# The gated mixing of a gMLP layer in float32r halves, its sample rows in one product over 96 rows

## The chip, the cores and the metric

The kernel runs on one core of a Trainium2 chip. The metric is the device time of one execution in microseconds; a smaller time is better. Times before are the median of three runs.

## The reference, cut to what matters

One inference step of a two-layer encoder over 256 prompt frames and 32 sample frames, 2048 wide. Layer 0 mixes tokens by a gated MLP, layer 1 by retention; each is followed by a SwiGLU feed-forward, and each of the four sublayers by a layer norm. The change lies in layer 0's mixer:

```python
z = jax.nn.gelu(x @ w_in, approximate=False)
u, v = jnp.split(z, 2, axis=-1)
v = layer_norm(v, ln_g, ln_b)
w = jnp.where(mask[None], w_s[:, :seg, :seg], 0.0)     # 8 groups, lower triangular
mixed = jnp.einsum('gts,bnsgc->bntgc', w, vg) + bias   # over the frames of one segment
s = u * mixed.reshape(bsz, t, GMLP_HALF)
return s @ w_out, v
```

A segment is 128 frames: the prompt has two, the sample is a short one of 32 frames. So for each of the 16 blocks of 128 channels there are three products: two of 128 by 128 frames and one of 32 by 32.

## The kernel before

All activations are kept transposed, with channels on the partitions and the 288 frames (256 prompt, 32 sample) along the free axis. The kernel works in float32 by halves: a value f is split into hi, its rounding to float32r, and lo = f - hi. `split` (L407) does this with one ScalarE copy (L408) and one VectorE subtraction (L409). Each 128x128 weight block then takes three float32r matmuls of 288 columns in `Core.step`: hi by x's hi (L98), hi by x's lo (L99), lo by x's hi (L100).

The weights come packed in the order in which they are used, in chunks of 8 blocks (512 KB each). `Core.prep` (L62) loads a chunk into `raw` by the SP queue, and splits it into `whi` and `wlo`. It runs three chunks ahead of use; `raw` has three buffers, `whi` and `wlo` four each. One chunk lasts TensorE 24 matmuls. TensorE's order is the program's order; that of ScalarE (ACT), VectorE (DVE), GpSimd (POOL) and the SP queue is set by a scheduler, and each of them works through its own list strictly in order.

A counter of finished column tiles ("ticks") places side work: `core.after(n, f)` runs f after n more tiles. Four PSUM banks hold column tiles in progress (`acc`), four more serve the side work (`aux`).

The gMLP layer, `gmlp` (L422), goes in this order:

- `tables` (L439) after tick 6: loads the mixing weights `ws` (8 groups, transposed), the mask, the biases, and multiplies mask into `ws` (L445).
- The first 16 column tiles of `a_in` give v. The first four are run as a group, so all four end almost together. `v_evac` (L452) applies Gelu (tile `vg`), transposes 32x32 pieces into `tv`, and after each four tiles `to_rows` (L412) moves the quarter through DRAM into rows: frames on the partitions, in `vp` (prompt, two segments) and `vs` (sample).
- `v_rows` takes statistics (L467), and `v_norm` (L482), once for each quarter of 512 channels, two ticks apart, normalises in place (L489 to L491).
- The next 16 column tiles give u (L497). Five ticks after each, `mix` (L500) forms the three products of its channel block in float32 (L505), adds the bias (L507), multiplies by u (L508) and splits the result into `sh` and `sl` (L511), which feed `a_out`.
- `tv` and `sl` share one piece of memory, `sl` being allocated in `mix(0)`.

`y` holds the input x at the start (it is split into `xh` and `xl`), and from `a_out` on the sums of the residual and layer norm (`PostNorm.part`, L207); in between it is unused.

Of the kernel before, what the change touches and what calls it, by code (L numbers as in the profile page):

```python
# [10 lines left out]
F32 = mybir.dt.float32  # L11
F32R = mybir.dt.float32r
# [7 lines left out]
P = 128  # L20
D = 2048
KT = D // P
NP = 256
NS = 32
NT = NP + NS
NX = NT + 2
NR = 3 * NS
# [132 lines left out]
def rsqrt(nc, out, v, t):  # L160

    nc.vector.tensor_scalar(out.bitcast(I32), v.bitcast(I32), -0.5, float(0x5F3759DF), ALU.mult, ALU.add)
    for _ in range(3):
        newton(nc, out, out, v, t)
# [242 lines left out]
def split(nc, hi, lo, f):  # L407
    nc.scalar.copy(hi, f)  # L408
    nc.vector.tensor_tensor(lo, f, hi.bitcast(F32), ALU.subtract)  # L409


def to_rows(nc, room, src, w, prompt, sample):  # L412


    blocks = room.rearrange("(b s) f -> s b f", s=32)
    for a in range(4):
        nc.gpsimd.dma_start(blocks[:, :, a * w:(a + 1) * w], src[32 * a:32 * a + 32, :, :])
    nc.gpsimd.dma_start(prompt, room[:NP, :].rearrange("(t p) f -> p t f", p=P))
    nc.gpsimd.dma_start(sample, room[NP:, :])


def gmlp(core, cst, x, y, lnp, ins, v_out):  # L422
    tc, nc = core.tc, core.nc
    xh, xl = x
    xs = lambda k: (xh[:, k, :NT], xl[:, k, :NT])
    with ExitStack() as es:
        pool = es.enter_context(tc.tile_pool(name="gm", bufs=1, reuse_waits="tile"))
        sh = pool.tile([P, KT, NT], F32R, name="g_sh")
        tv = pool.tile([P, 4, 9, 4, 32], F32, tag="sl", name="g_tv")
        vp = pool.tile([P, 2, D], F32, name="g_vp")  # L430
        vs = pool.tile([P, D], F32, name="g_vs")
        vt = [vp[:, 0, :], vp[:, 1, :], vs]
        st = pool.tile([P, 3, 4, 6], F32, name="g_st")
        bs = pool.tile([P, 8, NT], F32, name="g_bs")
        ws = pool.tile([P, 8, P], F32, name="g_ws")
        nrm = pool.tile([P, 3, 6], F32, name="g_nrm")
        mask = pool.tile([P, P], F32, name="g_mask")

        def tables():  # L439
            nc.sync.dma_start(ws, ins["wsT"])  # L440
            nc.sync.dma_start(mask, ins["mask"])
            nc.sync.dma_start(bs, ins["a_bs"])
            nc.sync.dma_start(cst["ln"], ins["lnv"])
            for g in range(8):
                nc.vector.tensor_tensor(ws[:, g, :], ws[:, g, :], mask, ALU.mult)  # L445

        core.after(6, tables)
        nc.gpsimd.memset(vs[NS:2 * NS, :], 0.0)
        nc.gpsimd.memset(vs[2 * NS:, :], 0.0)
        rows = [P, P, NS]  # L450

        def v_evac(m, ps):  # L452
            j = m - 16
            vg = pool.tile([P, NT], F32, tag="u", name=f"vg{j}", bufs=8)
            nc.scalar.activation(vg, ps[:, :NT], AF.Gelu)
            q, i = divmod(j, 4)
            nc.vector.transpose(tv[:, q, :, i, :], vg)
            if i == 3:
                t = tv[:, q, :, :, :].rearrange("p b i s -> p b (i s)")
                cs = slice(q * 512, (q + 1) * 512)  # L460
                to_rows(nc, core.room([NT, 512], f"g_room{q}"), t, P, vp[:, :, cs], vs[:NS, cs])
                core.after(2, lambda: v_rows(q))

        def v_rows(q):
            for t in range(3):
                n = rows[t]
                nc.vector.bn_stats(st[:n, t, q, :], vt[t][:n, q * 512:(q + 1) * 512])  # L467
            if q == 3:
                v_stats()

        def v_stats():
            for t in range(3):
                n = rows[t]
                mv = nrm[:n, t, 0:2]
                nc.vector.bn_aggr(mv, st[:n, t, :, :].rearrange("p a b -> p (a b)"))
                nc.vector.tensor_scalar(nrm[:n, t, 2:3], nrm[:n, t, 1:2], LN_EPS, None, ALU.add)
                rsqrt(nc, nrm[:n, t, 3:4], nrm[:n, t, 2:3], nrm[:n, t, 4:5])
                nc.vector.scalar_tensor_tensor(nrm[:n, t, 5:6], nrm[:n, t, 0:1], -1.0, nrm[:n, t, 3:4], ALU.mult, ALU.mult)
            for q in range(4):
                core.after(2 * q, lambda q=q: v_norm(q))  # L480

        def v_norm(q):  # L482
            cs = slice(q * 512, (q + 1) * 512)
            gb = pool.tile([P, 2, 512], F32, tag="gb", name=f"gb{q}", bufs=2)
            nc.sync.dma_start(gb, ins["a_gb"][:, :, cs])
            for t in range(3):
                n = rows[t]
                v = vt[t][:n, cs]
                nc.scalar.activation(v, v, AF.Identity, bias=nrm[:n, t, 5:6], scale=nrm[:n, t, 3:4])  # L489
                nc.vector.tensor_tensor(v, v, gb[:n, 0, :], ALU.mult)  # L490
                nc.vector.tensor_tensor(v, v, gb[:n, 1, :], ALU.add)  # L491
            if q == 3:
                nc.gpsimd.dma_start(v_out, vs[:NS, :])

        def u_evac(m, ps):
            u = pool.tile([P, NT], F32, tag="u", name=f"u{m}", bufs=8)
            nc.scalar.activation(u, ps[:, :NT], AF.Gelu)  # L497
            core.after(5 if m < 14 else 2, lambda: mix(m, u))

        def mix(m, u):  # L500
            g = m // 2
            ps = core.bank(f"mix{m}")
            for t in range(3):
                n = rows[t]
                nc.tensor.matmul(ps[:, t * P:t * P + n], vt[t][:, m * P:(m + 1) * P], ws[:, g, :n], start=True, stop=True)  # L505
            s = pool.tile([P, NT], F32, tag="s", name=f"s{m}", bufs=2)
            nc.vector.tensor_tensor(s, ps[:, :NT], bs[:, g, :], ALU.add)  # L507
            nc.vector.tensor_tensor(s, s, u, ALU.mult)  # L508
            if m == 0:
                late["sl"] = pool.tile([P, KT, NT], F32R, tag="sl", name="g_sl")  # L510
            split(nc, sh[:, m, :], late["sl"][:, m, :], s)  # L511

        late = {}
        core.tiles("a_in", 0, list(range(KT)), list(range(16, 32)), xs, v_evac, lag=0)
        core.tiles("a_in", 0, list(range(KT)), list(range(16)), xs, u_evac, grouped=False)
        ln = PostNorm(core, cst, x, y, lnp, 0)
        core.tiles("a_out", 0, list(range(KT)), list(range(KT)), lambda k: (sh[:, k, :], late["sl"][:, k, :]),
                   lambda m, ps: ln.last(m, ps, True))
    return ln
# [316 lines left out]
def hybrid_step(ctx, tc, ins, outs):  # L836
# [17 lines left out]
    for q in range(8):  # L854
# [4 lines left out]
        core.prep(min(q, 3))  # L859
    x = (xh, xl)  # L860
    ln = gmlp(core, cst, x, y, lnp, ins, outs["v"])
    ln = ffn(core, cst, x, y, lnp, 0, ln)
    ln = retention(core, cst, x, y, lnp, ln, ins, outs["st_p"], outs["st_s"])
# [88 lines left out]
```

## Time and profile before

| | |
|---|---|
| median of three runs | 2919.94 us (2919.65 to 2921.34) |
| profiled execution | 2918.83 us, span of its instructions 2917.0 us |
| granted TensorE clock | 0.999 |
| mixing products, L505 | 96 passes of TensorE, from 141.4 to 234.9 us |

A row of a group gives source line, engine, operation, tile names (out<-in), shape and count, then durations. PE is TensorE's matmul, PEld its weight load. A matmul's duration is its latency; matmuls overlap, so the cost of one in a stream is the time from its start to the next start. "idle before, releaser" names what ended the wait of an engine.

### The profile page before, as it was taken

The numbers are of one execution on the slowest core, as the hardware profiler recorded it, in microseconds if no ns is written. First come the engines' busy times: TensorE is split into PE (matmuls) and PEld (weight loads), VectorE is DVE, ScalarE is ACT, GpSimd is POOL, SyncE is SP. The second block draws the span as 40 slices with busy tenths as digits, with TensorE's granted clock in tenths as the row PEclk, the third lists the DMA queues.
The fourth block names the chain that finished last, engine by engine and source line by source line (L and its number), as shares of the span: only waits on it lengthen the run. The fifth ranks groups of instructions, "written<-read, shape, count | busy, mean of one in ns | idle before, by whom it ended". The sixth has DMA issues, their size and how long they took to land.

```text
span 2917.0 us, 51551 instructions
## 1 busy us (share of the span) xinstructions
PE 2903.5 (100%) x21592; PEld 2887.8 (99%) x21592; DVE 1709.3 (59%) x2493; ACT 1247.6 (43%) x1658; POOL 145.1 (5%) x242
## 2 busy tenths in 40 slices
PE   9999999999999999999999999999999999999998
PEld 9999999999999999999999999999999999999998
DVE  5667865444444456787755566767864444444455
ACT  5444544333333334564443444444553333333343
POOL 1100000000000000012200111200000000000001
PEclk9999999999999999999999999999999999999999
DMA  8654455555545545567655666655445554555553
GB/s 284 208 162 159 159 167 167 164 165 164 166 166 166 164 158 170 185 191 232 218 186 165 193 204 208 217 186 167 161 165 166 165 166 162 165 167 167 166 163 123
DMA packets 147305, 516.16 MB, mean 177 GB/s; under 512 B 18096, under 2 KB 21440, under 8 KB 146912
## 3 DMA queue, kind: packets, MB, share of 16 engines
q1 hardware_dynamic: 132704, 474.13, 49.5%
q0 software_dynamic: 14224, 38.59, 4.5%
q8 instruction: 169, 2.77, 0.4%
q14 instruction: 64, 0.52, 0.1%
q10 hardware_dynamic: 144, 0.15, 0.0%
HBM read 487.63 MB, written 25.17 MB: 176 GB/s over the span
## 4 chain that ended last, share of the span: by engine, by line
PE 99%; DVE 1%; DMA 0%; SPq 0%; ACT 0%; issue 0%; DVEq 0%; ACTq 0%
PE af_in L99 13%; PE af_in L98 13%; PE af_in L100 13%; PE ab_in L99 7%; PE ab_in L98 7%; PE ab_in L100 7%; PE af_out L98 6%; PE af_out L100 6%; PE af_out L99 6%; PE ab_out L100 2%; PE ab_out L99 2%; PE ab_out L98 2%; PE aa_in L98 2%; PE aa_in L100 2%; PE aa_in L99 2%; PE aa_out L98 1%
## 5 line engine op out<-in xcount | busy, mean ns | idle before, releaser
L409 DVE TENSOR_TENSOR wlo<-raw,whi 128x1024 fp32r<-128x1024 f32 (+1 forms) x894 | 1085.6, 1216 | 935.6 <-ACT whi L408 931.4
L408 ACT CAST whi<-raw 128x1024 fp32r<-128x1024 f32 (+1 forms) x894 | 930.8, 1043 | 1487.6 <-PE af_in L99 368.7
L99 PE MATMUL af_in<-xl,whi 128*128 128x288 f32 (+1 forms) x2816 | 833.0, 296 | 0.0
L98 PE MATMUL af_in<-xh,whi 128*128 128x288 f32 (+1 forms) x2816 | 832.9, 296 | 0.0
L100 PE MATMUL af_in<-xh,wlo 128*128 128x288 f32 (+1 forms) x2816 | 831.8, 295 | 0.0
L99 PEld LDWEIGHTS af_in<-xl,whi 128*128 128x128 f32 x2816 | 532.0, 189 | 0.0
L100 PEld LDWEIGHTS af_in<-xh,wlo 128*128 128x128 f32 x2816 | 531.6, 189 | 0.0
L98 PEld LDWEIGHTS af_in<-xh,whi 128*128 128x128 f32 x2816 | 531.1, 189 | 0.0
L99 PE MATMUL ab_in<-xl,whi 128*128 128x288 f32 (+1 forms) x1536 | 454.4, 296 | 0.7 <-DVE xl L409 0.7
L98 PE MATMUL ab_in<-xh,whi 128*128 128x288 f32 (+1 forms) x1536 | 455.0, 296 | 0.0
L100 PE MATMUL ab_in<-xh,wlo 128*128 128x288 f32 (+1 forms) x1536 | 453.6, 295 | 0.0
L98 PE MATMUL af_out<-hh,whi 128*128 128x288 f32 x1408 | 416.0, 295 | 0.0
L99 PE MATMUL af_out<-hl,whi 128*128 128x288 f32 x1408 | 415.1, 295 | 0.0
L100 PE MATMUL af_out<-hh,wlo 128*128 128x288 f32 x1408 | 414.4, 294 | 0.0
L99 PEld LDWEIGHTS ab_in<-xl,whi 128*128 128x128 f32 x1536 | 290.3, 189 | 2.0 <-DVE xl L409 0.9
L98 PEld LDWEIGHTS ab_in<-xh,whi 128*128 128x128 f32 x1536 | 289.6, 189 | 1.0
L100 PEld LDWEIGHTS ab_in<-xh,wlo 128*128 128x128 f32 x1536 | 289.9, 189 | 0.0
L100 PEld LDWEIGHTS af_out<-hh,wlo 128*128 128x128 f32 x1408 | 264.9, 188 | 0.0
L99 PEld LDWEIGHTS af_out<-hl,whi 128*128 128x128 f32 x1408 | 264.3, 188 | 0.0
L98 PEld LDWEIGHTS af_out<-hh,whi 128*128 128x128 f32 x1408 | 263.9, 187 | 0.0
L98 PE MATMUL aa_in<-xh,whi 128*128 128x288 f32 x512 | 152.5, 298 | 0.5 <-ACT whi L408 0.4
L100 PE MATMUL aa_in<-xh,wlo 128*128 128x288 f32 x512 | 151.6, 296 | 0.7 <-DVE wlo L409 0.7
(247 smaller groups left out, 2974.3 us busy)
## 6 DMA issues: line engine op xcount, KB each, us to landing
raw<-in_wpack_dram SPq DMA_DIRECT2D x886, 512.0 KB, 3.4
v_room<-tv POOLq DMA_DIRECT2D x32, 144.0 KB, 4.8
of<-o_room POOLq DMA_DIRECT2D x32, 144.0 KB, 4.4
vw<-v_room POOLq DMA_DIRECT2D x8, 512.0 KB, 5.6
out_st_s_dram<-sso POOLq DMA_DIRECT2D x16, 256.0 KB, 2.8
out_st_p_dram<-so POOLq DMA_DIRECT2D x16, 256.0 KB, 5.3
o_room<-to POOLq DMA_DIRECT2D x8, 512.0 KB, 3.8
y<-in_xT_dram SPq DMA_DIRECT2D x8, 288.0 KB, 6.1
```

The lines of the kernel that those rows point to most:

```text
L98: mm(ps[:, :n], hi, xh, start=first, stop=False)
L99: mm(ps[:, :n], hi, xl, start=False, stop=False)
L100: mm(ps[:, :n], lo, xh, start=False, stop=last)
L408: nc.scalar.copy(hi, f)
L409: nc.vector.tensor_tensor(lo, f, hi.bitcast(F32), ALU.subtract)
```

## The change

The mixing weights are split once into float32r halves `wh` and `wl`, and each prompt product becomes three float32r products (v hi by w hi, v hi by w lo, v lo by w hi). For the sample, the rows are stacked three times: `v3` holds v hi, v lo, v hi on 96 partitions and `w3` holds w hi, w hi, w lo, so that one product over 96 rows gives the same sum. v's halves for the prompt are written by `v_norm` into `sh` and `sl`, into the places that the gated product of the same channel block takes later; `sl` is allocated in `v_norm(0)`. v itself (`vp`) lies in `y`'s memory. The padding of `vs` to 128 rows and its two memsets go.

```diff
-        vp = pool.tile([P, 2, D], F32, name="g_vp")
-        vs = pool.tile([P, D], F32, name="g_vs")
+        vp = y.rearrange("p k n -> p (k n)")[:, :2 * D].rearrange("p (t f) -> p t f", t=2)
+        vs = pool.tile([NS, D], F32, name="g_vs")
+        v3 = pool.tile([NR, D], F32R, name="g_v3")
...
+        wh = pool.tile([P, 8, P], F32R, name="g_wh")
+        wl = pool.tile([P, 8, P], F32R, name="g_wl")
+        w3 = pool.tile([NR, 8, NS], F32R, name="g_w3")
...
                 nc.vector.tensor_tensor(ws[:, g, :], ws[:, g, :], mask, ALU.mult)
+            split(nc, wh, wl, ws)
+            for r in range(3):
+                src = wl.bitcast(F32) if r == 2 else ws
+                nc.scalar.copy(w3[r * NS:(r + 1) * NS], src[:NS, :, :NS])
...
-        nc.gpsimd.memset(vs[NS:2 * NS, :], 0.0)
-        nc.gpsimd.memset(vs[2 * NS:, :], 0.0)
...
         def v_norm(q):
             cs = slice(q * 512, (q + 1) * 512)
+            if q == 0:
+                late["sl"] = pool.tile([P, KT, NT], F32R, tag="sl", name="g_sl")
...
                 nc.vector.tensor_tensor(v, v, gb[:n, 1, :], ALU.add)
+                if t < 2:
+                    hi, lo = (r[:, 4 * q:4 * q + 4, t * P:(t + 1) * P] for r in (sh, late["sl"]))
+                    split(nc, hi, lo, v.rearrange("p (a f) -> p a f", a=4))
+                else:
+                    split(nc, v3[:NS, cs], v3[NS:2 * NS, cs], v)
+                    nc.scalar.copy(v3[2 * NS:, cs], v)
...
         def mix(m, u):
...
-            for t in range(3):
-                n = rows[t]
-                nc.tensor.matmul(ps[:, t * P:t * P + n], vt[t][:, m * P:(m + 1) * P], ws[:, g, :n], start=True, stop=True)
+            ms = slice(m * P, (m + 1) * P)
+            for t in range(2):
+                vh, vl = (r[:, m, t * P:(t + 1) * P] for r in (sh, late["sl"]))
+                for i, (v, w) in enumerate(((vh, wh), (vh, wl), (vl, wh))):
+                    nc.tensor.matmul(ps[:, t * P:(t + 1) * P], v, w[:, g, :], start=i == 0, stop=i == 2)
+            nc.tensor.matmul(ps[:, NP:NT], v3[:, ms], w3[:, g, :], start=True, stop=True)
...
-            if m == 0:
-                late["sl"] = pool.tile([P, KT, NT], F32R, tag="sl", name="g_sl")
             split(nc, sh[:, m, :], late["sl"][:, m, :], s)
```

## The prediction

> **What bounds the kernel now.** I read the page first: busy shares, granted clock, chain.
>
> ```profile
> span 2917.0 us, 51551 instructions
> PE 2903.5 (100%) x21592; PEld 2887.8 (99%) x21592; DVE 1709.3 (59%) x2493; ACT 1247.6 (43%) x1658; POOL 145.1 (5%) x242
> PEclk9999999999999999999999999999999999999999
> PE 99%; DVE 1%; DMA 0%; SPq 0%; ACT 0%; issue 0%; DVEq 0%; ACTq 0%
> ```
>
> TensorE is never idle, its clock is full, and 99% of the chain is PE. Second view, the waits of PE alone: all of them in the whole span.
>
> ```profile
> PE warm L853 <- POOL one L847: 1.0, 1, 1.0
> PE aa_in L100 <- DVE wlo L409: 0.7, 1, 0.7
> PE ab_in L99 <- DVE xl L409: 0.7, 1, 0.7
> PE aa_in L98 <- ACT whi L408: 0.4, 1, 0.4
> ```
>
> That is 2.8 us. So two things can move the time: how long PE needs for the mixing, and a new wait in PE's stream. The other engines matter only where they make PE wait. Third view, the timeline of PE around the first mixing product (start, duration, engine, line).
>
> ```profile
> 141.22 0.30 PE L100 MATMUL aa_in<-xh,wlo 128*128 128x288 f32 x1
> 141.36 0.61 PE L505 MATMUL mix<-g_ws,g_vp 128*128 128x128 f32 x4
> 141.80 0.31 PE L505 MATMUL mix<-g_ws,g_vs 128*128 128x32 f32 x2
> 141.94 0.38 PE L98 MATMUL aa_in<-xh,whi 128*128 128x288 f32 x1
> 142.16 0.30 PE L99 MATMUL aa_in<-xl,whi 128*128 128x288 f32 x1
> ```
>
> Three float32 products appear as six passes, two each. From the L100 before to the L99 behind are 0.94 us; two ordinary float32r products of 288 columns would take 2 x 0.133 (their start to start). The mixing therefore costs 0.67 us a column block, 0.111 a pass, and 16 x 0.67 = 10.7 us in all. That is everything on the path which the change can shorten.
>
> **Mixing on PE.** After: per block six float32r products of 128 columns and one of 96 rows by 32 columns, one pass each: seven instead of six. What does a short float32r pass cost? No row has one under 288 columns. A float32r pass takes 0.133 us at 288 columns and 0.230 at 512 (L805), so streaming alone is 0.433 ns a column plus 8 ns, or 0.064 us at 128. But each of these passes also loads 128 columns of weights. The weight loads beside the mixing:
>
> ```profile
> 141.69 0.30 PEld L505 LDWEIGHTS mix<-g_ws,g_vs 128*128 128x128 f32 x2
> 141.91 0.19 PEld L98 LDWEIGHTS aa_in<-xh,whi 128*128 128x128 f32 x1
> 142.03 0.19 PEld L99 LDWEIGHTS aa_in<-xl,whi 128*128 128x128 f32 x1
> ```
>
> The loads follow each other every 0.11 us even where the product has only 32 columns, and the float32r load at 141.91, behind such a short product, also keeps the next one 0.11 away. So I take 0.112 for all seven: 0.78 against 0.67, or +0.11 x 16 = **+1.8 us**. Bounds: 0.064 if the loads were hidden (6 x 0.064 + 0.031 = 0.42, -4.0 us), 0.133 if a short pass were no faster than a 288 one (0.93, +4.2 us). The load is the nearest row, hence 0.112. The Trainium skill (TensorE: Matmul & The Clock Gate, "Back-to-back issue gap") gives about 81 ns for a sustained load-and-multiply pair at 128 columns; by an estimate from it the seven would take 0.57 and this term would be -1.6 us. The six passes here keep 0.111, which speaks against it, but they are float32.
>
> **The tables (after tick 6).** Added: g_wh, a 128x1024 cast (L408 whi rows: 1.04), g_wl on DVE (1.22) and three 32x256 casts (about 0.40, whi 128x256 rows). In the changed program's ACT order g_wh stands ahead of the load of the Gelu table, and that ahead of the first vg. Before:
>
> ```profile
> 28.25 1.05 ACT L408 CAST whi<-raw 128x1024 fp32r<-128x1024 f32 x1 [1.64 <-DMA raw<-in_wpack_dram]
> 29.31 1.28 ACT L455 ACT_TABLE_LOAD   x1
> 30.47 1.09 DVE L445 TENSOR_TENSOR g_ws<-g_ws,g_mask 128x128 f32<-128x128 f32 x5
> 31.79 1.61 ACT L455 ACTIVATE vg<-aa_in 128x288 f32<-128x288 f32 x4 [1.19 <-PE aa_in L100]
> 32.78 0.29 PE L98 MATMUL aa_in<-xh,whi 128*128 128x288 f32 x1
> ```
>
> The table load used to lie in ACT's idle time. Now g_wh waits for the last mask product (31.56), ends at 32.64, the table is loaded by 33.94, the first vg ends at 34.36. All four accumulators are full by then, and PE's 32.78 product (the fifth column block) needs the bank that this vg frees: it starts at 34.4, **+1.6 us** for all that follows. Bounds: 0 if PE came late anyway, 2.6 with one more 1.0 us cast ahead. Behind g_wh also stand whi and wlo of blocks 10 to 12, 1 to 2 us later; the trace has them 3.9 to 7.5 us ahead of PE, and PE itself is 1.6 later: nothing. The load's 1.28 is followed within 0.02 us by the next ACT instruction in three of the trace's four. The Trainium skill (ScalarE: Activation LUTs, "What ACT_TABLE_LOAD costs") adds 1.38 us of drain to every switch; by an estimate from it the wait would be 3.0. The trace shows no such drain.
>
> **The splits of v.** Per 512-column quarter: on ACT two 128x512 and two 32x512 casts, on DVE three subtractions. The same shapes stand in retention:
>
> ```profile
> L408 ACT CAST vs<-vz x8: 610/612/615, 1241.6 to 1889.4; 32x512 fp32r<-32x512 f32 x8
> L409 DVE TENSOR_TENSOR vs<-vz,vs x8: 680/681/683, 1242.9 to 1891.0; 32x512 fp32r<-32x512 f32 x8
> ```
>
> Back to back DVE starts one every 0.605 us, so 12 x 0.605 = 7.3 us more for DVE and 16 x 0.52 = 8.3 for ACT (0.61 less the 0.09 by which neighbours overlap there), all of it in this stretch:
>
> ```profile
> 140.00:145.00 5.00, 5.00 (x41) 5.00 (x40) 5.00 (x9) 1.97 (x4) 0.00 (x0) 1.00 0.84 251
> 145.00:150.00 5.00, 5.00 (x40) 5.00 (x40) 3.49 (x6) 3.75 (x5) 0.00 (x0) 1.00 0.42 169
> ```
>
> The columns are PE, PEld, DVE, ACT, POOL busy. DVE is full from 125 to 145 and has 1.5 us free to 150. Weights are prepared three blocks ahead, and that cover is thinnest at block 45 (counted from 0): its wlo ended at 149.90, PE used it at 152.56, 2.66 us to spare. Counting DVE's order in the changed program, 24 instructions of 512 columns stand ahead of it since v_norm began, against 18: 6 x 0.605 = 3.6 us later, or 2.1 if the free 1.5 us is filled. PE comes 0.2 later too (two mixings). So between 0.8 to spare and a wait of 0.7; DVE now waits for ACT's casts in turn, so I lean to the late side: **+0.3 us**, range 0 to 2. If it is late, every further microsecond is PE's.
>
> **Edits at nothing.** The two memsets of vs (1.8 us each) ran on an idle POOL. Allocating g_sl in v_norm instead of mix 0 waits for the reads of g_tv, whose rows have landed before bn_stats at 124.8; v_norm's casts start at 129.6. v in y: x was split by 18.7, v lands from 50.6 on, y is written again only in a_out. The gated halves overwrite v's halves behind L507, which waited for the mixing anyway. The new wait, PE's mix 0 for the halves of quarter 0, is met some 4 us early (ready near 137.6, PE at 141.4 plus 1.6); the 24 products behind it in each block would pay if not. SP's order swaps one gb with one raw load, both waiting for the same buffers.
>
> **Sum.** 1.8 + 1.6 + 0.3 = +3.7 us. The profiled execution took 2918.83 (span 2917.0 and 1.8 around it), so 2922.5 on its terms; the median of the three runs is 1.1 above it: **2923.6 us**, +0.13%. A measurement of this kernel can tell about 0.2%, 5.8 us, from no change; so this is no change.
>
> **The rivals.**
> - The loads hide: short passes at 0.064. For it, the streaming rate of the long ones; against it, the 0.111 spacing. -4.0 + 1.6 + 1.0 (PE reaches block 45 earlier) = -1.4: 2918.5. Chance 0.13. By an estimate from the 81 ns of the Trainium skill (TensorE: Matmul & The Clock Gate, "Back-to-back issue gap") it would be 2920.5.
> - DVE falls behind at block 45, slower than before: if splits into four strided pieces take 0.95 instead of 0.605, or the ACT and DVE queues wait for each other at each step, the lateness is 5.5 instead of 3.6 and PE waits 2.5 more; from there on the total passes 5.8. About +6 to +9: 2926 to 2929. For it, a DVE that was full for 20 us; against it, that v_norm's DVE rows show no stretching. Chance 0.18.
> - Short float32r products are slow by themselves, as dear as a whole float32 product (0.222): 6 x 0.222 + 0.112 = 1.44 a block, +12.4, total +14: 2934. No row excludes it, none suggests it. Chance 0.12.
> - The change gains on PE beyond all this, by over 5.8 us: 0.03. The mixing would have to cost less than 0.3 us.
>
> **Numbers.** The forecast holds 0.54 (2921.5 to 2925.8). Same is the forecast and the hidden loads, 0.54 + 0.13 = 0.67; slower 0.18 + 0.12 = 0.30; faster 0.03. The range takes in the first two rivals and leaves out 0.15: 2918.5 to 2929.5.
>
> **What would show it.** In the profile after: seven mixing passes spaced 0.11 (right), 0.06 or 0.2 (wrong); one PE wait of about 1.6 us for ACT's vg near 33 us, with the table load at 32.7; PE waits for wlo near 154 us under 1 us. If the PE waits stay at 2.8 us in all, two of the three terms are wrong; if those near 154 pass 2.5, the second rival holds.

## The result, and the profile after

The changed kernel took 2924.41 us in the median (2923.57 to 2929.38, 21 runs), the kernel before 2919.89 us (2919.02 to 2921.68, 21 runs) beside it: ratio 1.0017, 95% interval 1.0011 to 1.0023. Together in a later measurement: 2924.94 against 2919.84, ratio 1.0016 [1.0007, 1.0025]. So +4.5 to +5.1 us (+4.8 by the means, both times), under the 0.2% (5.8 us) that the forecast called no change; the forecast was +3.7, 2923.6 us. Both intervals leave out 1: it is a small loss, not none. Differences below are made in two ways: medians against the median of the kernel before in the same measurement, and parts against before's profiled execution, by the start times of the same products. One thing is needed to read the medians: those of the kernel before range from 2919.8 to 2921.0, because its 101 executions beside the experiments lie in two groups, 50 around 2919.4 with a mean granted clock of 0.999 and 51 around 2921.1 with 0.998. Before's profiled execution, 2918.83, lies in the lower group, so the parts of a trace add up to more than the medians differ by.

The profiled execution of the change took 2926.21 us (span 2924.1), 1.8 above the median. Its page, the span, PE's busy time and the chain:

```profile
span 2924.1 us, 51630 instructions
PE 2907.6 (99%) x21608; PEld 2891.7 (99%) x21608; DVE 1719.0 (59%) x2506; ACT 1258.3 (43%) x1678; POOL 141.3 (5%) x240
PE 98%; DVE 1%; DMA 1%; ACT 0%; issue 0%; SPq 0%; DVEq 0%; ACTq 0%
```

PE has 16 more products (one pass more a block), and is still 98% of the chain. The timeline of PE around the first mixing:

```profile
146.07 0.30 PE L100 MATMUL aa_in<-xh,wlo 128*128 128x288 f32 x1
...
146.71 0.28 PE L521 MATMUL mix<-g_wh,g_sl 128*128 128x128 f32 x1
146.83 0.23 PE L522 MATMUL mix<-g_w,g_v 96*128 96x32 f32 x1
146.90 0.38 PE L98 MATMUL aa_in<-xh,whi 128*128 128x288 f32 x1
147.12 0.29 PE L99 MATMUL aa_in<-xl,whi 128*128 128x288 f32 x1
```

L100 to the L99 behind the mixing is 1.05 us where it was 0.94. From the second on, the seven passes start 0.109 to 0.113 us apart (the first two 0.06), and so do their weight loads, like the float32 passes before. By exact start times a block costs 0.78 us against 0.668: 16 x 0.113 = 1.8 us.

PE's waits have one new row in this execution, and the timeline near it shows what PE waited behind:

```profile
PE aa_in L98 <- ACT vg L461: 2.6, 1, 2.6
```

```profile
32.06 1.09 DVE L449 TENSOR_TENSOR g_ws<-g_ws,g_mask 128x128 f32<-128x128 f32 x5
33.18 1.04 ACT L408 CAST g_wh<-g_ws 128x1024 fp32r<-128x1024 f32 x1 [2.30 <-DVE g_ws L449]
34.25 1.28 ACT L461 ACT_TABLE_LOAD   x1
35.54 0.71 ACT L461 ACTIVATE vg<-aa_in 128x288 f32<-128x288 f32 x2
36.00 0.40 PE L98 MATMUL aa_in<-xh,whi 128*128 128x288 f32 x1 [2.64 <-ACT vg L461]
```

The order is the predicted one: cast of g_wh, table, first vg, PE. But it all stands 1.6 us later than before's rows had it: the last mask product ended at 33.15 in place of 31.56, for the most part because the mask had landed 1.4 us later (29.89 against 28.49). The wait put PE back by 2.8 us, where 1.6 was forecast. And something follows. Stretches of this execution (PE, PEld, DVE, ACT, POOL busy, granted clock, DMA share, GB/s):

```profile
39.00:40.00 1.00, 1.00 (x6) 1.00 (x6) 0.32 (x1) 0.98 (x1) 1.00 (x3) 0.50 0.68 132
42.00:45.00 3.00, 3.00 (x25) 3.00 (x24) 1.48 (x3) 0.78 (x2) 0.00 (x0) 1.00 1.01 388
```

For 3.41 us (37.54 to 40.95) the granted clock was 0.50: products of 288 columns started 0.240 apart instead of 0.133, and PE lost another 1.6 us.

So this execution is 7.1 us longer in its span: 0.4 at the start, 2.8 at the wait, 1.6 at half clock, 1.8 in the mixing, and 0.5 in rests of at most 0.3. One of these rests is in every trace with the seven passes (the change, e1, e5, e6, e7, e10): some 0.25 us near 245 us, where PE's L99 of `a_out` waits for the last block's `g_sl`.

The second profiled execution of the same kernel took 2925.50 us and is made up otherwise. It has no wait for vg. It lost 1.9 us in the first 22 us, in a stretch of half clock of its own; the first vg ended at 34.49 and PE came at 34.70. Instead PE waited later:

```profile
PE aa_in L100 <- DVE wlo L409: 2.3, 2, 1.5
```

One of the two is the wait of 0.7 us at the start, which every execution has. The other is at block 42 (blocks are counted from 0). In the timeline of this execution, with the wait, and of before, where the first of three wlo in a row ends at 140.19, 2.11 us ahead of PE:

```profile
144.75 1.20 DVE L409 TENSOR_TENSOR wlo<-raw,whi 128x1024 fp32r<-128x1024 f32 x1
...
146.01 0.40 PE L100 MATMUL aa_in<-xh,wlo 128*128 128x288 f32 x1 [1.53 <-DVE wlo L409]
```

```profile
138.98 3.48 DVE L409 TENSOR_TENSOR wlo<-raw,whi 128x1024 fp32r<-128x1024 f32 x3
142.30 0.30 PE L100 MATMUL aa_in<-xh,wlo 128*128 128x288 f32 x1
```

In the change PE lost 1.7 us there (1.82 from L99 to L100 instead of 0.13) and 0.3 at block 45. Its parts: 1.9 + 1.7 + 0.3 + 1.8, and 0.7 in rests, 6.4 in all.

### The profile page after: what moved, and what is told of

It reads as the page before. It is cut to its first block, busy times and chain, and to the rows that moved or that the text cites. A ratio compares the mean times of both kernels' runs of the same rounds, so it can differ in the third digit from the quotient of the medians.

```text
span 2924.1 us, 51630 instructions
## 1 busy us (share of the span) xinstructions
PE 2907.6 (99%) x21608; PEld 2891.7 (99%) x21608; DVE 1719.0 (59%) x2506; ACT 1258.3 (43%) x1678; POOL 141.3 (5%) x240
## 4 chain that ended last, share of the span: by engine, by line
PE 98%; DVE 1%; DMA 1%; ACT 0%; issue 0%; SPq 0%; DVEq 0%; ACTq 0%
PE af_in L99 13%; PE af_in L98 13%; PE af_in L100 13%; PE ab_in L99 7%; PE ab_in L98 7%; PE ab_in L100 7%; PE af_out L98 6%; PE af_out L100 6%; PE af_out L99 6%; PE ab_out L100 2%; PE ab_out L99 2%; PE ab_out L98 2%; PE aa_in L98 2%; PE aa_in L99 2%; PE aa_in L100 2%; PE aa_out L98 1%
## 5 line engine op out<-in xcount | busy, mean ns | idle before, releaser
L99 PE MATMUL af_in<-xl,whi 128*128 128x288 f32 (+1 forms) x2816 | 833.0, 296 | 0.0
L98 PE MATMUL af_in<-xh,whi 128*128 128x288 f32 (+1 forms) x2816 | 832.9, 296 | 0.0
L100 PE MATMUL af_in<-xh,wlo 128*128 128x288 f32 (+1 forms) x2816 | 831.8, 295 | 0.0
L99 PEld LDWEIGHTS af_in<-xl,whi 128*128 128x128 f32 x2816 | 532.1, 189 | 0.0
L100 PEld LDWEIGHTS af_in<-xh,wlo 128*128 128x128 f32 x2816 | 531.6, 189 | 0.0
L98 PEld LDWEIGHTS af_in<-xh,whi 128*128 128x128 f32 x2816 | 531.1, 189 | 0.0
L99 PE MATMUL ab_in<-xl,whi 128*128 128x288 f32 (+1 forms) x1536 | 454.4, 296 | 0.9 <-DVE xl L409 0.9
L98 PE MATMUL ab_in<-xh,whi 128*128 128x288 f32 (+1 forms) x1536 | 454.9, 296 | 0.0
L100 PE MATMUL ab_in<-xh,wlo 128*128 128x288 f32 (+1 forms) x1536 | 453.6, 295 | 0.0
L98 PE MATMUL af_out<-hh,whi 128*128 128x288 f32 x1408 | 416.0, 295 | 0.0
L99 PE MATMUL af_out<-hl,whi 128*128 128x288 f32 x1408 | 415.1, 295 | 0.0
L100 PE MATMUL af_out<-hh,wlo 128*128 128x288 f32 x1408 | 414.4, 294 | 0.0
L99 PEld LDWEIGHTS ab_in<-xl,whi 128*128 128x128 f32 x1536 | 290.3, 189 | 2.3 <-DVE xl L409 1.2
L98 PEld LDWEIGHTS ab_in<-xh,whi 128*128 128x128 f32 x1536 | 289.6, 189 | 1.0
L100 PEld LDWEIGHTS ab_in<-xh,wlo 128*128 128x128 f32 x1536 | 289.9, 189 | 0.0
L100 PEld LDWEIGHTS af_out<-hh,wlo 128*128 128x128 f32 x1408 | 265.0, 188 | 0.0
L99 PEld LDWEIGHTS af_out<-hl,whi 128*128 128x128 f32 x1408 | 264.3, 188 | 0.0
L98 PEld LDWEIGHTS af_out<-hh,whi 128*128 128x128 f32 x1408 | 263.9, 187 | 0.0
L98 PE MATMUL aa_in<-xh,whi 128*128 128x288 f32 x512 | 153.6, 300 | 3.2 <-ACT vg L461 2.6
L100 PE MATMUL aa_in<-xh,wlo 128*128 128x288 f32 x512 | 152.4, 298 | 0.7 <-DVE wlo L409 0.7
```

The lines of the kernel that those rows point to most:

```text
L98: mm(ps[:, :n], hi, xh, start=first, stop=False)
L99: mm(ps[:, :n], hi, xl, start=False, stop=False)
L100: mm(ps[:, :n], lo, xh, start=False, stop=last)
```

## The experiments

Theory: the change costs 1.8 us in the mixing (seven passes of 0.11), a wait for the first vg behind the early halves of the mixing weights, and, where v's splits have used up the cover (the time by which a block's wlo is ready before PE needs it), a wait for wlo; PE's lateness from one cause covers the next. Rivals: all of it is in the mixing; or v's splits cost nothing; or the half clock comes by itself.

**e1_halves_late.** The mask products and the halves move behind v's seventh tile:

```diff
+        def halves(vg):
+            nc.vector.scalar_tensor_tensor(mask, vg[:, :P], 0.0, mask, ALU.mult, ALU.add)
+            for g in range(8):
+                nc.vector.tensor_tensor(ws[:, g, :], ws[:, g, :], mask, ALU.mult)
+            split(nc, wh, wl, ws)
...
+            if j == 6:
+                halves(vg)
```

> The changed kernel, but the mask products and the halves of the mixing weights wait for v's seventh tile (the mask is multiplied by data of that tile in between, with the factor 0), so that they stand behind the Gelu table's load. Theory (the changed kernel loses 1.8 us in the mixing's seven passes and the rest by the wait for the first vg, with the half clock behind it): no PE wait for vg, no slice of half clock after the start, and 2919.9 + 1.8 = 2921.7 us, 2.7 below the changed kernel's median. Rival (the splits of v, or the late halves themselves, cost the rest): still 2924 or more. Rival (the half clock comes by itself in every execution of this program): no wait for vg, but a stretch at 0.5 and about 2923.3.

Measured: 2923.25 us (2920.96 to 2925.24, 11 runs), the kernel before 2921.01 beside it: +2.2, ratio 1.0008 [0.9999, 1.0017]. The profiled execution took 2921.60: no wait for vg, full clock from 5.2 us on, the mixing at 0.78, and no other part above 0.5. The lowest time, 2920.96, is the lowest of the kernel before in this measurement (2918.90) plus 2.1. So the early halves are what the vg wait and the half clock at 37.5 come from: no trace with late halves (e1, e4, e5, e7, e8, e8_again) has that wait, and none has a stretch of half clock at 37.5, so the third rival is out for this stretch; those near 15 us are another matter, told in the last section. The median lies 1.6 above the 2921.7 that I gave; 1.1 of it is the median of before, which is that much higher in this measurement, and 0.4 is left.

**e2_table_halves_alone.** The kernel before plus the halves of the weights, unused.

```diff
+            w4 = ws.rearrange("p (k a) n -> p k a n", a=2)
+            wh, wl = (sh[:, k:k + 4, :2 * P].rearrange("p k (a n) -> p k a n", a=2) for k in (0, 4))
+            split(nc, wh, wl, w4)
+            for r in range(3):
+                nc.scalar.copy(sh[r * NS:(r + 1) * NS, 8, :2 * P].rearrange("p (g n) -> p g n", g=8), ws[:NS, :, :NS])
```

> The kernel before, with one part of the change: after the mask products it also makes the halves of the mixing weights and the three small casts, written where nothing reads them; the mixing itself stays in three float32 products and v is not split. Theory: the same wait for the first vg as in the changed kernel, 1.6 to 2.8 us, and a stretch of half clock when the wait is near 2.9: 1.6 to 4.4 us above the kernel before, 2921.5 to 2924.3; the mixing stays at 0.67 us a block. Rival (everything comes from the mixing and the splits of v): 2919.9, as before.

Measured: 2921.30 us (2920.71 to 2923.51), +0.3, ratio 1.0005 [0.9996, 1.0014]. The median says "nothing", the mean +1.3, the lowest time +1.8 (before: 2918.90). In the profiled execution there is no wait for vg at all: PE was 3.8 us late from the start (a stretch of half clock of 6.8 us), the first vg ended at 36.38 and PE came at 36.57. So in this execution the price of the early halves is not added to the late start, it is hidden behind it. Both theory and rival were too simple.

**e6_gelu_table_early.** The changed kernel with one instruction more at the start:

```diff
+    tc.keep_in_program_order(nc.scalar.preload_act_table_set("gelu_and_others"))
```

> The changed kernel with the Gelu table loaded at the start, so that no table load stands between the cast of the mixing weights and the first vg. Theory: the first vg ends 1.28 us earlier, PE's wait for it is 1.3 to 1.5 us instead of 2.8, no half clock behind it: 1.3 to 2.9 below the changed kernel, 2921.5 to 2923.1 us. If the cast alone made PE wait (the load ran beside something else): the wait stays near 2.8 and the time near 2924.4.

Measured: 2923.52 us (2922.04 to 2925.75), +2.5, ratio 1.0011 [1.0002, 1.0020]. That is above the 2921.5 to 2923.1 that I gave. Its lowest time is 1.1 above that of e1 and 0.8 to 1.5 below those of the change, so it seems that part of the wait goes with the table's 1.28; its trace cannot show it. The profiled execution started 2.2 us late, had no wait for vg, and lost 1.7 us at block 42 and 0.3 at block 45, as the second execution of the change.

**e3_float32_mixing.** The changed kernel, mixing in float32 products, the sample over its 32 rows; the halves are made and not read.

```diff
+            for t in range(3):
+                n = rows[t]
+                nc.tensor.matmul(ps[:, t * P:t * P + n], vt[t][:n, m * P:(m + 1) * P], ws[:n, g, :n], start=True, stop=True)
...
```

> The changed kernel with its mixing put back to three float32 products (six passes); the halves of v and of the weights are still made but not read. Theory: the mixing is back at 0.67 us a block, 16 x 0.114 = 1.8 us less than the changed kernel, 2922.6 us; the wait for vg stays. Rival (the passes cost the same, and what the changed kernel loses lies in the casts and waits): 2924.4, no difference.

Measured: 2926.37 us (2925.63 to 2928.43), +5.4, ratio 1.0022 [1.0013, 1.0031]: slower than the change, where 1.8 us less was expected. A block costs 0.975 us. The wait for vg, which I had expected to stay, is not in its profiled execution, which started 2.2 us late. The kernel before ran the sample's product over 128 rows, padded with zeros; I had cut it to 32. **e9_before_32_rows** tells whether that is it:

```diff
-  vt[t][:, m * P:(m + 1) * P], ws[:, g, :n]
+  vt[t][:n, m * P:(m + 1) * P], ws[:n, g, :n]
```

> The kernel before with one edit: the sample's float32 product in the mixing reads 32 rows of v and of the weights instead of 128 (the other 96 are zeros in the kernel before). Theory: a float32 product over 32 rows between products over 128 rows costs 0.31 us a block more, as in the experiment with the float32 mixing (0.975 against 0.668): 16 x 0.307 = 4.9 us above the kernel before. Rival (the 0.31 came from something else there, such as v lying in y's memory): the mixing stays at 0.668 and the time at the kernel before's.

Measured: 2924.47 us against 2920.64, +3.8, ratio 1.0014 [1.0005, 1.0023]. Its timeline:

```profile
142.28 0.30 PE L100 MATMUL aa_in<-xh,wlo 128*128 128x288 f32 x1
142.41 0.61 PE L505 MATMUL mix<-g_ws,g_vp 128*128 128x128 f32 x4
142.95 0.40 PE L505 MATMUL mix<-g_ws,g_vs 32*128 32x32 f32 x2
143.28 0.40 PE L98 MATMUL aa_in<-xh,whi 128*128 128x288 f32 x1
```

A block costs 0.975 us here too: 0.205 from the last 128-row pass to the first of 32 rows, and 0.201 from the last of 32 rows to L98, against 0.11 for a pass among 128-row ones; the two passes of 32 rows start 0.133 apart, against 0.031 in the kernel before. In this trace that is 16 x 0.307 = 4.9 us by the blocks, of which 4.6 are left in the start times behind the mixing. The Trainium skill (TensorEngine Tiling (Array Packing), "Key Properties") says that a change of tiling mode drains TensorE; the gap on both sides of the 32-row product agrees, but it covers 0.18 of the 0.31 us, and why the two passes themselves stand further apart is open. The product over 96 rows shows no such gap: the L98 behind it starts 0.08 us later.

**e7_no_v_halves.** e1 without the splits of v; the mixing reads x's halves, which have the same shape, so its result is not the layer's.

```diff
-                    split(nc, hi, lo, v.rearrange("p (a f) -> p a f", a=4))
...
-                    split(nc, v3[:NS, cs], v3[NS:2 * NS, cs], v)
-                    nc.scalar.copy(v3[2 * NS:, cs], v)
...
-                vh, vl = (r[:, m, t * P:(t + 1) * P] for r in (sh, late["sl"]))
+                vh, vl = (r[:, m, t * P:(t + 1) * P] for r in (xh, xl))
...
-            nc.tensor.matmul(ps[:, NP:NT], v3[:, ms], w3[:, g, :], start=True, stop=True)
+            nc.tensor.matmul(ps[:, NP:NT], xh[:NR, m, :P], w3[:, g, :], start=True, stop=True)
```

> The kernel with the late halves of the mixing weights (e1), without the splits of v: the mixing's seven products read the halves of x, which have the same shape, in place of those of v. PE's work is the same; DVE has 7.3 us less to do and ACT 8.3. Theory: the mixing keeps 0.78 us a block; wlo of blocks 42 and 45 are over 2 us ahead of PE again, no execution waits there, and the time is the kernel before's plus 1.8, with a narrower spread than e1's: about 1 us below e1. Rival (v's splits cost nothing): the same time and spread as e1.

Measured: 2921.62 us (2920.96 to 2923.28), the kernel before 2919.84: +1.8, ratio 1.0006 [0.9997, 1.0015]. The mixing stays at 0.78 a block; wlo of block 42 is 2.55 us ahead of PE and that of block 45 4.02 (0.42 and 0.05 in e1). No wait for wlo and the time are as expected; the distance to e1, each against its own before, is 0.4 us where about 1 was expected.

**e10_early_halves_no_v.** The changed kernel with the same edit as e7, so with the halves of the weights made early, in `tables`:

```diff
-                    split(nc, hi, lo, v.rearrange("p (a f) -> p a f", a=4))
...
-                vh, vl = (r[:, m, t * P:(t + 1) * P] for r in (sh, late["sl"]))
+                vh, vl = (r[:, m, t * P:(t + 1) * P] for r in (xh, xl))
...
```

> The changed kernel without the splits of v (the mixing reads the halves of x, as in e7), the halves of the mixing weights made early, as in the change: with the changed kernel, e1 and e7 it completes the square of early or late halves, with or without v's splits. Theory: the early halves alone cost the wait for vg, 1.6 to 2.8 us, where PE is not late at the start, and nothing where it is 2 us late already; no wait for wlo in any execution. So above e7 (before + 1.8) by 0.3 to 2 us in the median, its fastest runs by about 1.6: median before + 2 to + 4, none under 2922. Rival (the early halves cost only by shifting DVE, whose cover at blocks 42 and 45 v's splits have used up): without those splits the time is e7's, before + 1.8, with runs from 2921.0 on.

Measured: 2923.34 us (2922.91 to 2925.98), the kernel before 2920.73: +2.6, ratio 1.0012 [1.0003, 1.0021]; no run under 2922.9. Its profiled execution starts only 0.5 us late and shows the wait for vg on its own:

```profile
PE aa_in L98 <- ACT vg L460: 1.9, 1, 1.9
```

PE lost 2.1 us there; the clock stayed full. The rival, e7's time, is out. The four corners of the square, median minus the median of before in the same measurement, in brackets the same of the means, and the lowest run (e10 ran on another chip than e1, e7 and the later measurement of the change):

| halves of the weights | with v's splits | without |
|---|---|---|
| early | +4.5, +5.1 (+4.8, +4.8); 2923.57, 2922.88 (the change) | +2.6 (+3.7); 2922.91 (e10) |
| late | +2.2 (+2.4); 2920.96 (e1) | +1.8 (+1.9); 2920.96 (e7) |

The lowest run is set by the halves alone: 2 us. v's splits leave it as it is and raise the middle: by the means 0.5 with late halves and 1.1 with early ones; the medians, which jump between the groups, say 0.4 and about 2. The intervals of the ratios reach 2.6 us to either side, so that the times alone don't tell the two corners of a row apart; the traces at block 42 do. The granted clocks of the single executions fit the hiding: e10's four at 0.999 have a median of 2923.6 and its seven at 0.998 one of 2923.3, e7's eight at 0.999 one of 2921.6 and its three at 0.998 one of 2923.2. By these few executions the early halves cost 2 us at the higher clock and nothing at the lower; where in them the clock fell is not on record.

**e5_v_halves_twice.** e1 with every split of v made twice.

```diff
...
+                    for _ in range(2):
                         split(nc, hi, lo, v.rearrange("p (a f) -> p a f", a=4))
...
```

> The kernel with the late halves of the mixing weights (e1), in which every split of v is made twice: 12 more subtractions on DVE (7.3 us) and 16 more casts on ACT (8.3 us), nothing more on PE. Theory (v's splits have used up the cover: in e1's execution wlo of block 42 was 0.42 us and that of block 45 0.05 us ahead of PE): 3 of the doubled subtractions stand ahead of block 42's wlo and 6 ahead of block 45's, so PE waits 3 x 0.605 - 0.4 = 1.4 us at block 42 and 6 x 0.605 - 1.4 = 2.2 more at block 45, 3.6 in all or somewhat more behind: 3 to 5 us above e1. Rival (DVE has room enough; the small rests in e1 are chance): the same time as e1 and no wait for wlo.

Measured: 2931.11 us (2928.75 to 2932.72, 5 runs) against 2919.84, +11.3, ratio 1.0038 [1.0024, 1.0052]: 9 above e1, where 3 to 5 were expected. The rival, room enough on DVE, is out. The waits of PE, and the stretches at block 42:

```profile
PE aa_in L100 <- DVE wlo L409: 6.3, 3, 5.0
```

```profile
142.00:145.00 3.00, 0.61 (x5) 0.37 (x4) 3.00 (x6) 3.00 (x6) 0.00 (x0) 1.00 0.00 0
145.00:148.00 3.00, 0.39 (x1) 0.39 (x2) 2.91 (x4) 2.90 (x6) 0.00 (x0) 0.50 0.50 173
```

Both DVE (third figure) and ACT (fourth) are full: the wait for wlo at block 42 is 5.2 us instead of the 1.4 that I had counted from DVE's subtractions. ACT's casts stand in the same chain, and I had not counted them. The clock falls to 0.50 for 6.8 us in that wait, and PE lost another 2.0 us.

**e4_five_passes.** e1, with v's high half against both halves of the weights in one product of 256 columns, the two sums added on DVE.

```diff
...
+                nc.tensor.matmul(ps[:, o:o + 2 * P], vh, whl[:, g, :, :].rearrange("p a n -> p (a n)"), start=True, stop=False)
+                nc.tensor.matmul(ps[:, o:o + P], vl, wh[:, g, :], start=False, stop=True)
...
```

> The kernel with the late halves of the mixing weights (e1), the mixing in five float32r passes instead of seven: v's high half meets both halves of the weights in one product of 256 columns, the sums of the two are added on DVE (two more additions a block, the sample's in a bank of its own). Theory: a pass costs 0.112 up to about 256 columns (256 x 0.433 ns + 8 ns = 0.119): 2 x 0.119 + 3 x 0.112 = 0.57 a block, 3.4 us below e1, 1.6 below the kernel before, if DVE's additions leave its cover at blocks 42 and 45 alone (they start behind block 45). Rival (the streaming of 256 columns adds to the load): 0.79 a block, no gain on e1.

Measured: a block costs 0.572 us, as expected, but the time is 2922.59 us against 2920.64, +2.0, ratio 1.0007 [0.9998, 1.0016]. In its profiled execution wlo of block 45 came late (DVE had waited 1.35 us for an ACT cast of v), PE lost 2.1 us at 153, and another 1.5 at half clock, 3.4 us long, behind that. In this execution the gain in the mixing went into that wait; 3.4 us below e1 had been expected.

**e8_float32_prompt_96_rows** and **e8_again.** The prompt's products in float32 as before, the sample alone in halves over 96 rows, its halves made late.

```diff
...
+                nc.tensor.matmul(ps[:, t * P:(t + 1) * P], vt[t][:, ms], ws[:, g, :], start=True, stop=True)
             nc.tensor.matmul(ps[:, NP:NT], v3[:, ms], w3[:, g, :], start=True, stop=True)
```

> The two 128-column products of each mixing back in float32 (two passes each), the sample alone in the 96-row product of float32r halves; only the sample's rows of v and a 32x32 corner of the mixing weights are split, late as in e1. Theory (a pass costs its 0.111 us of weight load whatever its type): five passes, 0.556 us a block, 16 x 0.112 = 1.8 us below the kernel before; 4 more subtractions on DVE (2.4 us) fit into its cover. Rival (what made the 32-row float32 product of the experiment before dear, 0.31 us a block, is a change of rows between products): 96 rows behind 128 cost the same, 0.87 us a block, 3 us above the kernel before.

> The kernel with the prompt's products in float32 and the sample's over 96 rows (e8) once more. Theory: 0.56 us a block, 1.8 us below the kernel before, as in its first runs (1.9). Rival (the 1.9 was the mix of executions with and without a stretch of half clock at the start): no difference, or above.

Measured: 2917.90 us (2916.97 to 2920.76) against 2919.84, ratio 0.9993 [0.9985, 1.0002], and 2918.02 (2917.38 to 2920.50) against 2920.64, ratio 0.9992 [0.9984, 1.0001]. The timeline of the second:

```profile
141.80 0.30 PE L100 MATMUL aa_in<-xh,wlo 128*128 128x288 f32 x1
141.94 0.61 PE L518 MATMUL mix<-g_ws,y 128*128 128x128 f32 x4
142.30 0.26 PE L519 MATMUL mix<-g_w,g_v 96*128 96x32 f32 x1
142.41 0.38 PE L98 MATMUL aa_in<-xh,whi 128*128 128x288 f32 x1
```

As expected, five passes, 0.555 us a block, 16 x 0.113 = 1.8 us less than before (1.8 by the means too, both times): the 96 rows cost no more than their pass. In the second trace wlo of blocks 42 and 45 is 1.3 and 2.0 us ahead of PE. These are the lowest medians of all, 6.5 to 7 us under the change; against the kernel before, both intervals just take in 1.

**after_again.** The changed kernel, shown above.

> The changed kernel as it is, a further execution with a profile, on the chip of the three above. Theory: its time is set by whichever is latest: PE's start (2 us later in executions with a stretch of half clock there), the wait for vg near 33 us (shorter by what the start is late), and wlo of block 42, which follows v's landing 12 to 15 us behind its last transpose. So the three parts do not add up: 2 to 4.5 us above the kernel before, and the wait for vg is 2.8 us or less, by as much less as PE is late at the 100th product.

Measured, as shown above: +5.1, a little over the 2 to 4.5 us that I gave; no wait for vg in an execution that started 1.9 us late, as expected.

## Why the prediction was right or wrong

- **Mixing, +1.8: right.** Seven passes at 0.112 were 0.78 a block in every trace that has them. The doubt between 0.064, 0.112 and 0.133 a pass is settled for the row of the weight loads; the 81 ns of the Trainium skill (TensorE: Matmul & The Clock Gate, "Back-to-back issue gap") do not fit these float32r passes. e8 shows the same price from the other side: one pass fewer than before is 1.8 us less.
- **The tables, +1.6: right in place and order, wrong as one number.** It was 2.8 and 0 in the two executions of the change and 2.1 in e10. It grows by what the last mask product ends later (1.6 us in the first) and shrinks by what PE is late already. The lowest runs put it near 2 (2923 against 2921). The bound of 0 "if PE came late anyway" was in the text, but I took before's single profile for PE's place. No drain of 1.4 us shows behind the table load: vg started 0.01 us behind it.
- **Half clock behind the wait: missing.** 1.6 us in the first execution. No term of the sum had the thought that a wait costs clock too.
- **DVE at block 45, +0.3: the mechanism right, the place and the size not.** Block 42 is the thin one, and before's trace already has it so: its wlo is 2.11 us ahead of PE, that of block 45 2.66, which the prediction called the thinnest. Three of the new subtractions stand ahead of block 42's wlo, which ends 16.8 us behind v's last landing in the change and 15.4 without the splits (e7). What the step took from one trace, the landing itself, varies: it came 12.3 us behind v's last transpose in one execution of the change and 15.1 in the other. With 12.3 nothing waits, with 15.1 PE waits 2.0. The lateness named in the second rival is thus real, at another block, and stays short of its +6 (six splits at 0.95 are 5.7 us late, not the 5.5 given there).
- **Edits at nothing.** No trace shows a wait at the memsets, v in y's memory, g_sl's new place or mix 0. What the list lacks is the 0.25 us at the last block's g_sl.
- **The total.** 3.7 forecast, 4.5 and 5.1 measured. The terms 1.6 and 0.3 gave too little, and it stayed close because the parts replace each other: whoever is late first hides the next. The prediction added them up, so that the sum came this near is in part luck; a single execution's parts come to 6.4 and 7.1.

Open: why v lands 2.8 us later in some executions. Both traces with 15.1 us have early halves and a late start, but e2 and e3 have these too and landed after 13.1 and 12.8 us. A collision with the weights' loads is possible and was not tried.

## What to carry to other kernels

Where PE is busy throughout, count the passes: at 128 columns and fewer a float32 pass and a float32r pass cost the same 0.11 us, so three float32r products are one pass dearer than one float32 product with its two, while one product over 96 rows in place of those two saves one. Work put ahead of a table load, or into an engine that is full for 20 us, is priced not by its duration but by the cover that is left, and that cover moves from execution to execution by the landing of a DMA: take it from more than one trace. Waits at different places of one stream do not add up, so test them in a square of with and without. Where the times lie in groups, look at the lowest runs, the means and the granted clock beside the median.

## What the runs showed of the hardware

- **A wait of under 3 us halves the clock afterwards, if it falls into one window.** The clock records change only at steps that are multiples of 3.41 us apart in each trace. Idle time of PE (from start to start, less 0.13 for the product itself) in the 3.41 us ahead of a fall: 1.88 in the change's first execution, 2.23 in e4, 2.53 in e5. Without a fall: 1.42 in after_again, 1.45 in e6, and e10's wait of 2.1, of which 1.2 lie in the fuller window. The starts fit in: the two waits near 12 us, for whi and wlo, came to 1.9 to 2.3 us of one such window in the executions whose clock fell there (e2, e3, e6, e8, after_again), and to 1.6 or less in those where it did not (the kernel before, e1, e4, e5, e7, e9, e10, e8_again and the change's first), partly because the window's edge lay between them. So in 14 traces the point lies between 1.6 and 1.9 us of 3.41, without an exception; no run set the idle time on purpose. In e2 the clock stayed at half for a second window with only 1.0 us idle, so the way back may ask for more. One window at half clock costs 1.4 to 1.6 us in these traces, besides the waits ahead of it. That such a stretch parts the two groups of the kernel before fits their clocks: one window at 0.50 takes 0.0006 off the mean of a span of 2917 us, and all 51 executions at 0.998 took 2920.26 us or more, all 50 at 0.999 2920.50 or less. No profile of the upper group exists, so where in it the clock falls is not shown. The mean on record is not always that of the work: e8's profiled execution has 0.949 throughout, with the products of 288 columns 0.133 apart as elsewhere. The Trainium skill (TensorE: Matmul & The Clock Gate, "What's actually happening") describes such a free-running window of 3413 ns, and the steps agree; its advice in "Why this matters for your kernels", no gaps over about 3 us, is too wide here.
- **A float32 product over 32 rows among 128-row ones costs 0.31 us more than one over 128** (e3, e9); one over 96 rows costs its pass of 0.11 and no more (e8).
